# Two-operand work on the mixer's constants: from GpSimd to VectorE, one instruction per weight slot

## The chip, the cores and the metric

One core of a Trainium2 chip runs the whole program. The metric is the device time of one execution in microseconds (us). Engines are called by the names of the profile: PE is TensorE (PEld its weight loads), DVE is VectorE, ACT is ScalarE, POOL is GpSimd, SP the queue that issues the weight loads.

## What is computed

One inference step of two layers for 272 prompt and 32 sample tokens (304 columns in layer 0). Layer 0 mixes by a gated short convolution, layer 1 by a state-space mixer with complex diagonal state; each is followed by an MLP.

```python
def sq_relu_mlp(x, w_up, w_down):
    h = jax.nn.relu(x @ w_up)          # 2048 -> 8192
    return (h * h) @ w_down            # 8192 -> 2048

# constants of the state-space mixer, from weights alone:
dt = jnp.exp(log_step)[:, None]
mag = jnp.exp(lr * dt)
abar_re, abar_im = mag * jnp.cos(li * dt), mag * jnp.sin(li * dt)
q_re = ((abar_re - 1) * lr + abar_im * li) / (lr * lr + li * li)
q_im = (abar_im * lr - (abar_re - 1) * li) / (lr * lr + li * li)
bbar_re = q_re[..., None] * b_re - q_im[..., None] * b_im
bbar_im = q_re[..., None] * b_im + q_im[..., None] * b_re
```

The kernel runs the mixer over blocks of four tokens, and for this needs powers of `abar` and their products with `bbar` and with C. It makes them while the first MLP runs, and stores them to DRAM in the layouts in which layer 1 reads them.

## The kernel before

All weights stream through `WeightStream` (lines 40 to 82) as 704 slots, each one pair of 128x512 tiles (512 KB). For a slot, SP loads `raw` (4 buffers), ACT copies it to `whi` (L66; fp32r, a rounded copy), DVE makes `wlo = raw - whi` (L68); both have 3 buffers and are made two slots ahead (`LOOK = 2`). `group` (from line 172) then issues 24 matmuls for the slot: 4 output tiles x 2 contraction tiles x 3 products (L196 and L197 with `whi`, L198 with `wlo`). A group gathers 4 output tiles in 4 of the 7 PSUM buffers `ps`; in its first slot it leaves the matmuls of the fourth tile to the end, behind the 18 of the other three, since that tile's buffer must first be freed by an eviction of the group before.

The first MLP has 256 slots. Eight column parts `f` of the hidden layer are worked off, part f up before part f-1 down, so that the order is 32 slots up, then 16 down and 16 up in turn, and at the end 16 twice down. Counted from 0, slots 32 to 47 are down, 48 to 63 up, 64 to 79 down, and so on every 32. An up group has 8 slots, a down group 4. Evictions of a finished group run in the first slots of the next: for up, `ev_up` has DVE make `zt` (L836) and `at` (L838), ACT the rounded `hid` (L732), DVE the rest (L733); for down, `h_add` (L794) adds to `h` on DVE. The first of them is issued ahead of the first slot's `whi` and `wlo`, the others one per slot in the middle of it.

The background list `bg` holds the work on the mixer's constants (`prep_tasks`, from line 443), behind 8 empty items. At the end of every slot of the first MLP, `group` takes one item (lines 222 to 232): `None` does nothing, a function is called, and a generator is advanced by one `yield`. In the kernel before, the call that makes a generator uses up a slot of its own. Engines work their instructions in the order of issue; so what an item issues on DVE or ACT stands behind that slot's `wlo` and evictions and ahead of the next slot's. The items in their order: load (`t_alloc`), `exp`, sine and cosine and `abar` on DVE (`t_exp`, `t_trig`, `t_abar`), scaling of B by the norm (`t_wnorm`, L550), powers (`t_pow` by `cmul`, L518 to L523), `a4` by PE transposes (`t_a4`). Then for each of two halves (real, imaginary): four `t_w` of three operations on 128x1024 (L584 to L586), four transposing copies on ACT (`t_wm`, L592), stores to `d_b` and `d_m1` issued by POOL (L596, L601). Then C is loaded and half of it negated (`t_cload`, `t_cneg`), and four sets follow, each with a copy and four `t_m2` of three operations on 128x512 (L636, L640 to L642) and stores to `d_c` and `d_m2` (L648, L651). The profile calls all of these DRAM tensors `d_m`, `d_b`, `d_c`, the SBUF buffers `prep` and `nat`. At the end come 256 small matmuls on the constants (`t_kmm`, L688, 16 in an item), `t_d` (L696, L698, on POOL) and stores to `d_t` (L701).

The views of `t_w` and `t_m2`, whose inputs lie differently:

```python
b = [bg_[:, x * 1024:(x + 1) * 1024].rearrange("g (p c) -> g p c", c=16) for x in range(2)]
e = [nat(16 + 2 * tau + x).unsqueeze(2).to_broadcast([P, 64, 16]) for x in range(2)]

c = [bg_[:, x * 1024:(x + 1) * 1024].rearrange("g (c p) -> g p c", c=16)[:, ps_, :] for x in range(2)]
a = [nat(8 + 2 * (i - 1) + x)[:, ps_].unsqueeze(2).to_broadcast([P, 32, 16]) for x in range(2)]
```

`t_w` reads B with neighbouring elements; `t_m2` reads C with a step of 64 elements; both broadcast one factor along the innermost 16.

Of the kernel before, what the change touches and what calls it, by code (L numbers as in the profile page):

```python
# [11 lines left out]
AF = mybir.ActivationFunctionType  # L12
ALU = mybir.AluOpType
# [3 lines left out]
P = 128  # L17
# [62 lines left out]
def build(ctx, tc, I, O, dbg=None):  # L80
    nc = tc.nc
    V, S, G, T = nc.vector, nc.scalar, nc.gpsimd, nc.tensor
# [62 lines left out]
    bg = []  # L145
# [42 lines left out]
    def group(kts, rhs, n, rate=1, fast=False, each=None):  # L188

        ps = [psum() for _ in range(4)]  # L190

        def mm(m, kk, si, hi, lo):
            xh, xl = rhs(kts[si + kk])
            o = ps[m][:, :n]
            wh, wl = hi[:, kk, m * P:(m + 1) * P], lo[:, kk, m * P:(m + 1) * P]
            T.matmul(out=o, lhsT=wh, rhs=xh, start=si == 0 and kk == 0, stop=False)  # L196
            T.matmul(out=o, lhsT=wh, rhs=xl, start=False, stop=False)  # L197
            T.matmul(out=o, lhsT=wl, rhs=xh, start=False, stop=si + 2 >= len(kts) and kk == 1)  # L198

        for si in range(0, len(kts), 2):  # L200
            while si == 0 and len(tasks) > 3 and tasks[3][2]:
                tasks.pop(0)[1]()
            run_pend()
            hi, lo = W.take()
            if si + 2 >= len(kts):
                order = [(m, kk) for m in range(4) for kk in range(2)]
            else:
                order = [(m, kk) for kk in range(2) for m in range(4 if si else 3)]
                if si == 0:
                    order += [(3, 0), (3, 1)]  # L210
            for m, kk in order[:4]:
                mm(m, kk, si, hi, lo)
            pop_tasks(rate)
            if each is not None:
                each()
            for m, kk in order[4:]:
                mm(m, kk, si, hi, lo)
            if len(tasks) > 5 or fast:
                pop_tasks(rate)
            else:  # L220
                run_pend()
            if bg:
                f = bg[0]
                if hasattr(f, "__next__"):
                    if next(f, bg) is bg:
                        bg.pop(0)
                else:
                    bg.pop(0)
                    if f is not None:
                        it = f()  # L230
                        if hasattr(it, "__next__"):
                            bg.insert(0, it)
        return ps

# [33 lines left out]
    big = rp.tile([P, 12000], F32, tag="BIG", name="big")  # L268
# [178 lines left out]
    def prep_tasks():  # L447
# [9 lines left out]
        def nat(i, n=64):  # L457
            return st["vy"][:, i * 64:i * 64 + n]
# [56 lines left out]
        def cmul(o, a, b):  # L515

            t = nat(4)
            G.tensor_tensor(out=nat(o), in0=nat(a), in1=nat(b), op=ALU.mult)  # L518
            G.tensor_tensor(out=t, in0=nat(a + 1), in1=nat(b + 1), op=ALU.mult)
            G.tensor_tensor(out=nat(o), in0=nat(o), in1=t, op=ALU.subtract)  # L520
            G.tensor_tensor(out=nat(o + 1), in0=nat(a), in1=nat(b + 1), op=ALU.mult)
            G.tensor_tensor(out=t, in0=nat(a + 1), in1=nat(b), op=ALU.mult)
            G.tensor_tensor(out=nat(o + 1), in0=nat(o + 1), in1=t, op=ALU.add)  # L523
# [21 lines left out]

        def t_wnorm():

            for o, n in ((st["big"][:, 0:2048], 128), (nat(30, 16), 1)):
                v = o.rearrange("g (p c) -> g p c", c=16)
                G.tensor_tensor(out=v, in0=v, in1=nat(31, 16).unsqueeze(1).to_broadcast([P, n, 16]), op=ALU.mult)  # L550

        def t_pow():
            cmul(10, 8, 8)
            cmul(12, 10, 8)
            cmul(14, 10, 10)
            for n in range(1, 4):
                cmul(16 + 2 * n, 14 + 2 * n, 8)

        def t_a4():
            ps = psum1()  # L560
# [11 lines left out]
                V.tensor_copy(out=a4[sl, 3, :], in_=im)  # L572

        L += [t_exp, t_trig, t_abar]
        L.extend([t_wnorm, t_pow, None, None, None, None, None, None, None, None, t_a4])

        def t_w(ri, tau):
            bg_ = st["big"]
            b = [bg_[:, x * 1024:(x + 1) * 1024].rearrange("g (p c) -> g p c", c=16) for x in range(2)]
            tmp = bg_[:, 2048:3072].rearrange("g (p c) -> g p c", c=16)  # L580
            wb = bg_[:, 3072:7168].rearrange("g (p t c) -> g p t c", t=4, c=16)
            e = [nat(16 + 2 * tau + x).unsqueeze(2).to_broadcast([P, 64, 16]) for x in range(2)]
            o = wb[:, :, tau, :]
            G.tensor_tensor(out=o, in0=b[ri], in1=e[0], op=ALU.mult)  # L584
            G.tensor_tensor(out=tmp, in0=b[1 - ri], in1=e[1], op=ALU.mult)
            G.tensor_tensor(out=o, in0=o, in1=tmp, op=ALU.subtract if ri == 0 else ALU.add)  # L586

        def t_wm(ri, tau):
            bg_ = st["big"]
# [14 lines left out]
        for ri in range(2):  # L604
            for tau in range(4):
                L.append(lambda ri=ri, tau=tau: t_w(ri, tau))
                L += [None, None]
            L += [None]
            for tau in range(4):
                L.append(lambda ri=ri, tau=tau: t_wm(ri, tau))  # L610
            L += [None, lambda ri=ri: t_wout(ri)]
            L += [lambda ri=ri, a=a: t_m1out(ri, a) for a in range(4)]
            L += [None] * 6
# [5 lines left out]

        def t_cneg():  # L620
            bg_ = st["big"]
            G.tensor_scalar(out=bg_[:, 1024:2048], in0=bg_[:, 1024:2048], scalar1=-1.0, scalar2=None, op0=ALU.mult)

        L.extend([t_cload, None, None, None, t_cneg])

# [4 lines left out]
        def t_m2(ri, hf, i):  # L630
            bg_ = st["big"]
            ps_ = slice(hf * 32, hf * 32 + 32)
            c = [bg_[:, x * 1024:(x + 1) * 1024].rearrange("g (c p) -> g p c", c=16)[:, ps_, :] for x in range(2)]
            o = cbuf(ri, hf)[:, :, i, :]
            if i == 0:
                G.tensor_copy(out=o, in_=c[ri])  # L636
                return
            tmp = bg_[:, 2048:2560].rearrange("g (p c) -> g p c", c=16)
            a = [nat(8 + 2 * (i - 1) + x)[:, ps_].unsqueeze(2).to_broadcast([P, 32, 16]) for x in range(2)]
            G.tensor_tensor(out=o, in0=c[ri], in1=a[0], op=ALU.mult)  # L640
            G.tensor_tensor(out=tmp, in0=c[1 - ri], in1=a[1], op=ALU.mult)
            G.tensor_tensor(out=o, in0=o, in1=tmp, op=ALU.add if ri == 0 else ALU.subtract)  # L642

        def t_m2out(ri, hf, a):
            cb = cbuf(ri, hf)
# [740 lines left out]
```

## Time and profile before

| | |
|---|---|
| median of 3 runs | 2549.51 us (2547.49 to 2554.91) |
| the profiled execution | 2551.72 us, span 2549.9 us |
| mean granted clock of PE | 0.987 of full speed |
| first MLP in the trace | 469.4 us to about 1390 us |

The profile's page gives busy time by engine, the span in 40 slices and the costliest groups. The trace answers for any stretch, line or engine; in its lists of instructions, the bracket at a line's end is the idle time of the engine ahead of the instruction and what ended it. A busy PE is not PE at its peak: its records overlap, so that matmuls per stretch and the granted clock say more than the busy share.

### The profile page before, as it was taken

Reading aid. Unit: us, or ns where it says so; the run is one execution under the profiler, and the core shown is the slowest. Engines: PE = TensorE matmul, PEld = TensorE weight load, DVE = VectorE, ACT = ScalarE, POOL = GpSimd, SP = SyncE. Lnnn points to the kernel's source line nnn. Section 1 sums busy time; section 2 is a strip of 40 time slices with the busy share of each in tenths; the row PEclk is TensorE's granted clock in tenths of the full one; section 3 lists DMA queues with packets and bytes.
Section 4 is the critical chain, followed back from the end, with each engine's and each line's share of the span. In section 5 each row is a group of like instructions: output and inputs, shape, how many; then the busy total and the mean of one; then the engine's idle time right before and its main releaser. Section 6 shows DMA issues by size and latency. Waiting matters only on the chain.

```text
span 2549.9 us, 43295 instructions
## 1 busy us (share of the span) xinstructions
PE 2457.9 (96%) x18078; PEld 2433.5 (95%) x18078; DVE 1469.3 (58%) x2012; ACT 968.1 (38%) x1230; POOL 369.6 (14%) x440
## 2 busy tenths in 40 slices
PE   6999999999989999999989889999999999999998
PEld 5999999999989999999989789999999999999998
DVE  4644555667565774545456983556555545555555
ACT  3333334432424333333323644444333333333334
POOL 2000001016233880000027013000000000000000
PEclk9999999999999999999999999999999999999999
DMA  6555555555656777555569754555555555555554
GB/s 146 154 159 159 160 160 170 157 157 150 174 133 199 209 195 238 160 166 169 162 145 189 139 146 132 166 165 162 170 163 169 163 169 167 166 166 166 165 166 112
DMA packets 256353, 418.17 MB, mean 164 GB/s; under 512 B 64484, under 2 KB 68260, under 8 KB 255980
## 3 DMA queue, kind: packets, MB, share of 16 engines
q1 hardware_dynamic: 248448, 389.62, 52.1%
q0 software_dynamic: 7648, 25.73, 4.9%
q8 instruction: 142, 2.33, 0.4%
q14 instruction: 55, 0.45, 0.1%
q10 hardware_dynamic: 60, 0.05, 0.0%
HBM read 392.71 MB, written 22.63 MB: 163 GB/s over the span
## 4 chain that ended last, share of the span: by engine, by line
PE 58%; DVE 2%; DMA 1%; issue 1%; POOL 0%; ACT 0%; DVEq 0%; ACTq 0%; POOLq 0%
PE ps L196 18%; PE ps L198 18%; PE ps L197 18%; PE ps L1121 1%; DMA raw<-in_mlp_w_down 1%; PE px L688 1%; PE ps L1112 0%; DMA ssm_big<-d_m 0%; DVE ssm_tb L1045 0%; PE ps L1350 0%; DVE wlo L68 0%; DVE ssm_xr L1051 0%; DVE ssm_tb L1046 0%; DVE ssm_xr L1049 0%; PE ps L969 0%
## 5 line engine op out<-in xcount | busy, mean ns | idle before, releaser
L68 DVE TENSOR_TENSOR wlo<-raw,whi 128x1024 fp32r<-128x1024 f32 x701 | 908.7, 1297 | 934.2 <-ACT whi L66 933.5
L66 ACT ACTIVATE whi<-raw 128x1024 fp32r<-128x1024 f32 x704 | 743.2, 1057 | 1034.4 <-PE ps L197 874.7
L196 PE MATMUL ps<-hid,whi 128*128 128x304 f32 (+1 forms) x2048 | 615.8, 301 | 22.8 <-DVE h L794 19.7
L198 PE MATMUL ps<-hid,wlo 128*128 128x304 f32 (+1 forms) x2048 | 615.1, 300 | 9.5 <-DVE wlo L68 9.4
L197 PE MATMUL ps<-hid,whi 128*128 128x304 f32 (+1 forms) x2048 | 615.2, 300 | 0.0
L198 PE MATMUL ps<-xs_m,wlo 128*128 128x304 f32 (+1 forms) x2048 | 611.1, 298 | 1.6 <-DVE wlo L68 1.5
L196 PE MATMUL ps<-xs_m,whi 128*128 128x304 f32 (+1 forms) x2048 | 610.3, 298 | 0.0
L197 PE MATMUL ps<-xs_m,whi 128*128 128x304 f32 (+1 forms) x2048 | 610.2, 298 | 0.0
L196 PEld LDWEIGHTS ps<-hid,whi 128*128 128x128 f32 x2048 | 389.3, 190 | 25.2 <-DVE h L794 20.9
L198 PEld LDWEIGHTS ps<-hid,wlo 128*128 128x128 f32 x2048 | 389.7, 190 | 11.2 <-DVE wlo L68 11.2
L197 PEld LDWEIGHTS ps<-hid,whi 128*128 128x128 f32 x2048 | 388.9, 190 | 0.0
L198 PEld LDWEIGHTS ps<-xs_m,wlo 128*128 128x128 f32 x2048 | 384.6, 188 | 2.4 <-DVE wlo L68 2.4
L196 PEld LDWEIGHTS ps<-xs_m,whi 128*128 128x128 f32 x2048 | 384.6, 188 | 1.2
L197 PEld LDWEIGHTS ps<-xs_m,whi 128*128 128x128 f32 x2048 | 384.5, 188 | 0.1
L196 PE MATMUL ps<-xs,whi 128*128 128x304 f32 x768 | 233.5, 304 | 6.0 <-DVE h L388 6.0
L198 PE MATMUL ps<-xs,wlo 128*128 128x304 f32 x768 | 233.2, 304 | 0.0
L197 PE MATMUL ps<-xs,whi 128*128 128x304 f32 x768 | 232.6, 303 | 0.0
L732 ACT ACTIVATE hid<-at 128x304 fp32r<-128x304 f32 (+1 forms) x128 | 57.8, 452 | 309.8 <-DVE at L838 309.8
L196 PEld LDWEIGHTS ps<-xs,whi 128*128 128x128 f32 x768 | 145.7, 190 | 6.4 <-DVE h L388 6.3
L198 PE MATMUL ps<-g,wlo 128*128 128x288 f32 x512 | 151.1, 295 | 0.0
L196 PE MATMUL ps<-g,whi 128*128 128x288 f32 x512 | 151.1, 295 | 0.0
L197 PE MATMUL ps<-g,whi 128*128 128x288 f32 x512 | 150.7, 294 | 0.0
(283 smaller groups left out, 2450.7 us busy)
## 6 DMA issues: line engine op xcount, KB each, us to landing
raw<-in_mlp_w_up SPq DMA_DIRECT2D x256, 512.0 KB, 3.7
raw<-in_mlp_w_down SPq DMA_DIRECT2D x256, 512.0 KB, 3.6
raw<-in_conv_w_in SPq DMA_DIRECT2D x96, 512.0 KB, 3.8
raw<-in_conv_w_out SPq DMA_DIRECT2D x32, 512.0 KB, 3.6
raw<-in_ssm_glu_w_b SPq DMA_DIRECT2D x32, 512.0 KB, 3.6
raw<-in_ssm_glu_w_a SPq DMA_DIRECT2D x32, 512.0 KB, 3.6
ssm_big<-d_m SPq DMA_DIRECT2D x64, 128.0 KB, 3.0
d_m<-prep POOLq DMA_DIRECT2D x16, 256.0 KB, 8.9
```

What stands on the lines that cost most here:

```text
L66: self.nc.scalar.activation(out=hi, in_=r, func=AF.Copy)
L68: eng.tensor_tensor(out=lo, in0=r, in1=hi.bitcast(F32), op=ALU.subtract)
L196: T.matmul(out=o, lhsT=wh, rhs=xh, start=si == 0 and kk == 0, stop=False)
L197: T.matmul(out=o, lhsT=wh, rhs=xl, start=False, stop=False)
L198: T.matmul(out=o, lhsT=wl, rhs=xh, start=False, stop=si + 2 >= len(kts) and kk == 1)
L688: T.matmul(out=ps[:16, g % 8 * 64:(g % 8 + 1) * 64], lhsT=wl[:, g, :], rhs=cl[:, g, :], start=True, stop=True)
L732: S.activation(out=dh, in_=src, func=AF.Copy)
L1121: T.matmul(out=ps[:NK, n // 2 * P:(n // 2 + 1) * P], lhsT=ssm["SH"][pi][:, 0:NK, n % 2, tl * 4 + n // 2], rhs=ssm["m2"][t % 3][:, n, :], s ...
```

## The change

All two-operand work on the constants up to and with `t_m2` is issued on DVE (`V`) in place of POOL (`G`), `t_cneg` and the copies of `t_m2` on ACT (`S`). The functions become generators that `yield` so that a slot gets about one DVE instruction (two in every second slot of `t_m2`, six small ones in a slot of `t_pow`). A generator now runs its first piece in the slot in which it is made, and many empty items go. The K matmuls and all behind them come 3 slots earlier. DMA issues, memsets and `t_d` stay on POOL.

```diff
                         it = f()
-                        if hasattr(it, "__next__"):
+                        if hasattr(it, "__next__") and next(it, bg) is not bg:
                             bg.insert(0, it)
...
         def cmul(o, a, b):
             t = nat(4)
-            G.tensor_tensor(out=nat(o), in0=nat(a), in1=nat(b), op=ALU.mult)
+            V.tensor_tensor(out=nat(o), in0=nat(a), in1=nat(b), op=ALU.mult)
...
         def t_wnorm():
-            for o, n in ((st["big"][:, 0:2048], 128), (nat(30, 16), 1)):
+            for o, n in ((st["big"][:, 0:1024], 64), (st["big"][:, 1024:2048], 64), (nat(30, 16), 1)):
                 v = o.rearrange("g (p c) -> g p c", c=16)
-                G.tensor_tensor(out=v, in0=v, in1=nat(31, 16).unsqueeze(1).to_broadcast([P, n, 16]), op=ALU.mult)
+                V.tensor_tensor(out=v, in0=v, in1=nat(31, 16).unsqueeze(1).to_broadcast([P, n, 16]), op=ALU.mult)
+                if n > 1:
+                    yield
 
         def t_pow():
...
+            for o, a, b in ((10, 8, 8), (12, 10, 8), (14, 10, 10), (18, 16, 8), (20, 18, 8), (22, 20, 8)):
+                cmul(o, a, b)
+                if o != 22:
+                    yield
...
-        L.extend([t_wnorm, t_pow, None, None, None, None, None, None, None, None, t_a4])
+        L.extend([t_wnorm, t_pow, None, t_a4])
...
-            G.tensor_tensor(out=o, in0=b[ri], in1=e[0], op=ALU.mult)
-            G.tensor_tensor(out=tmp, in0=b[1 - ri], in1=e[1], op=ALU.mult)
-            G.tensor_tensor(out=o, in0=o, in1=tmp, op=ALU.subtract if ri == 0 else ALU.add)
+            V.tensor_tensor(out=o, in0=b[ri], in1=e[0], op=ALU.mult)
+            yield
+            V.tensor_tensor(out=tmp, in0=b[1 - ri], in1=e[1], op=ALU.mult)
+            yield
+            V.tensor_tensor(out=o, in0=o, in1=tmp, op=ALU.subtract if ri == 0 else ALU.add)
...
                 L.append(lambda ri=ri, tau=tau: t_w(ri, tau))
-                L += [None, None]
...
-            G.tensor_scalar(out=bg_[:, 1024:2048], in0=bg_[:, 1024:2048], scalar1=-1.0, scalar2=None, op0=ALU.mult)
+            S.activation(out=bg_[:, 1024:2048], in_=bg_[:, 1024:2048], func=AF.Copy, scale=-1.0)
...
             if i == 0:
-                G.tensor_copy(out=o, in_=c[ri])
+                S.activation(out=o, in_=c[ri], func=AF.Copy)
                 return
...
-            G.tensor_tensor(out=o, in0=c[ri], in1=a[0], op=ALU.mult)
-            G.tensor_tensor(out=tmp, in0=c[1 - ri], in1=a[1], op=ALU.mult)
-            G.tensor_tensor(out=o, in0=o, in1=tmp, op=ALU.add if ri == 0 else ALU.subtract)
+            V.tensor_tensor(out=o, in0=c[ri], in1=a[0], op=ALU.mult)
+            yield
+            V.tensor_tensor(out=tmp, in0=c[1 - ri], in1=a[1], op=ALU.mult)
+            V.tensor_tensor(out=o, in0=o, in1=tmp, op=ALU.add if ri == 0 else ALU.subtract)
...
                     L.append(lambda ri=ri, hf=hf, i=i: t_m2(ri, hf, i))
-                    L.append(None)
+                    L += [None] * (i == 0)
```

The items by slot, from walking the list of each kernel:

| item | before | after |
|---|---|---|
| `t_wnorm`, `t_pow` | 30, 31 | 27 to 29, 30 to 35 |
| `t_w`, real half | 41 to 50 (every third) | 38 to 49 |
| `t_wm`, real half | 54 to 57 | 51 to 54 |
| `t_w`, imaginary half | 70 to 79 (every third) | 67 to 78 |
| `t_wm`, imaginary half | 83 to 86 | 80 to 83 |
| `t_m2`, operations of sets 1 to 4 | 106 to 112, 120 to 126, 134 to 140, 148 to 154 | 103 to 110, 117 to 124, 131 to 138, 145 to 152 |
| first K matmuls | 179 | 176 |

The slot is that in which an item is issued. POOL has nothing there that waits for the slot; it works off its instructions as soon as their inputs are ready.

## Rows read from the trace of the kernel before

**Rows 1.** The page's busy line: engine, busy us, share of the span, instructions.
```profile
PE 2457.9 (96%) x18078; PEld 2433.5 (95%) x18078; DVE 1469.3 (58%) x2012; ACT 968.1 (38%) x1230; POOL 369.6 (14%) x440
```

**Rows 2.** Waits of PE, 390 to 1350 us: us in total, times, longest us.
```profile
PE ps L196 <- DVE h L794: 19.7, 5, 7.3
PE ps L198 <- DVE wlo L68: 10.9, 7, 3.0
PE ps L196 <- DVE zt L836: 2.4, 1, 2.4
```

**Rows 3.** Stretches: length, busy PE, PEld, DVE, ACT, POOL; clock; DMA share, GB/s.
```profile
590.00:600.00 10.00, 5.48 (x30) 5.24 (x30) 9.48 (x6) 3.41 (x4) 9.92 (x5) 0.82 0.33 106
...
800.00:810.00 10.00, 10.00 (x74) 10.00 (x73) 5.31 (x7) 3.94 (x5) 1.13 (x2) 1.00 0.93 276
...
830.00:840.00 10.00, 6.29 (x40) 5.80 (x39) 9.44 (x8) 2.79 (x5) 9.84 (x7) 0.94 0.27 84
...
1000.00:1100.00 100.00, 100.00 (x723) 100.00 (x722) 52.80 (x68) 34.70 (x39) 0.00 (x0) 1.00 0.52 159
```

**Rows 4.** Timeline, 582 to 612 us: start, us, engine, line, operation [idle ahead].
```profile
585.97 2.96 DVE L68 TENSOR_TENSOR wlo<-raw,whi 128x1024 fp32r<-128x1024 f32 x1
...
593.60 2.95 DVE L68 TENSOR_TENSOR wlo<-raw,whi 128x1024 fp32r<-128x1024 f32 x1
595.55 3.22 POOL L586 TENSOR_TENSOR prep<-prep 128x1024 f32<-128x1024 f32 x1
...
596.99 0.62 PE L196 MATMUL ps<-hid,whi 128*128 128x304 f32 x1 [4.52 <-DVE h L794]
```

**Rows 5.** DVE groups, 697 to 725 us, then 1000 to 1100: busy us, mean ns.
```profile
L68 DVE TENSOR_TENSOR wlo<-raw,whi 128x1024 fp32r<-128x1024 f32 x5 | 11.7, 2347 | 6.0 <-ACT whi L66 6.0
...
L68 DVE TENSOR_TENSOR wlo<-raw,whi 128x1024 fp32r<-128x1024 f32 x30 | 36.8, 1226 | 42.6 <-ACT whi L66 42.6
L794 DVE TENSOR_TENSOR h<-h,ps 128x304 f32<-128x304 f32 x14 | 6.5, 465 | 0.0
```

**Rows 6.** Instructions by tile and line: durations min/median/max ns, first and last start.
```profile
L196 PE MATMUL ps<-xs_m,whi x2048: 288/297/528, 469.4 to 2428.3; 128*128 128x304 f32 x94, 128*128 128x288 f32 x93
...
L688 PE MATMUL px<-prep x256: 219/219/230, 1109.0 to 1290.9; 128*16 128x64 f32 x128
```

**Rows 7.** DVE groups of the whole span, by shape: busy us, mean ns.
```profile
L1084 DVE TENSOR_TENSOR ssm_tb<-ssm_tb,ssm_big 128x640 f32<-128x640 f32 x6 | 4.9, 819 | 0.0
...
L485 DVE SCALAR_TENSOR_TENSOR nat<-nat 128x64 f32<-128x64 f32 x7 | 1.6, 223 | 0.2
```

**Rows 8.** Timeline of DVE in an up group's first slots, 1000 to 1060 us.
```profile
1017.10 1.23 DVE L68 TENSOR_TENSOR wlo<-raw,whi 128x1024 fp32r<-128x1024 f32 x1 [0.47 <-ACT whi L66]
...
1020.70 1.23 DVE L68 TENSOR_TENSOR wlo<-raw,whi 128x1024 fp32r<-128x1024 f32 x1 [0.47 <-ACT whi L66]
```

**Rows 9.** Timelines of ACT and PE, 664 to 680 us: `whi` behind `t_wm`.
```profile
670.21 1.05 ACT L66 ACTIVATE whi<-raw 128x1024 fp32r<-128x1024 f32 x1
...
675.77 1.04 ACT L66 ACTIVATE whi<-raw 128x1024 fp32r<-128x1024 f32 x1
...
678.12 0.19 PEld L198 LDWEIGHTS ps<-xs_m,wlo 128*128 128x128 f32 x1 [0.27 <-DVE wlo L68]
```

**Rows 10.** ACT groups of the whole span, by shape: busy us, mean ns.
```profile
L66 ACT ACTIVATE whi<-raw 128x1024 fp32r<-128x1024 f32 x704 | 743.2, 1057 | 1034.4 <-PE ps L197 874.7 <-issue 59.9 <-DMA raw<-in_mlp_w_down 46.8
...
L592 ACT ACTIVATE prep<-prep 128x1024 f32<-128x1024 f32 x8 | 16.6, 2076 | 0.0
```

**Rows 11.** Transfers that write or read `prep`, issue to landing.
```profile
DMA to landing us min/median/max: 2.6/9.4/20.1
```

**Rows 12.** Timeline of ACT behind two bursts of stores: `whi` and its wait.
```profile
694.88 1.06 ACT L66 ACTIVATE whi<-raw 128x1024 fp32r<-128x1024 f32 x1 [5.72 <-DMA raw<-in_mlp_w_down]
...
959.68 1.06 ACT L66 ACTIVATE whi<-raw 128x1024 fp32r<-128x1024 f32 x1 [6.10 <-DMA raw<-in_mlp_w_down]
```

**Rows 13.** Timeline of ACT behind the stores to `d_t`: `whi` and its wait.
```profile
1321.98 1.06 ACT L66 ACTIVATE whi<-raw 128x1024 fp32r<-128x1024 f32 x1 [11.28 <-DMA raw<-in_mlp_w_down]
```

More of the change, by code (lines that the diff above doesn't have):

```diff
@@ L517, in cmul @@
             t = nat(4)
-            G.tensor_tensor(out=nat(o), in0=nat(a), in1=nat(b), op=ALU.mult)
[L519 to L523, printed above, removed]
+            V.tensor_tensor(out=nat(o), in0=nat(a), in1=nat(b), op=ALU.mult)
+            V.tensor_tensor(out=t, in0=nat(a + 1), in1=nat(b + 1), op=ALU.mult)
+            V.tensor_tensor(out=nat(o), in0=nat(o), in1=t, op=ALU.subtract)
+            V.tensor_tensor(out=nat(o + 1), in0=nat(a), in1=nat(b + 1), op=ALU.mult)
+            V.tensor_tensor(out=t, in0=nat(a + 1), in1=nat(b), op=ALU.mult)
+            V.tensor_tensor(out=nat(o + 1), in0=nat(o + 1), in1=t, op=ALU.add)
         def t_abar():
@@ L546, in t_wnorm @@
         def t_wnorm():
-            for o, n in ((st["big"][:, 0:2048], 128), (nat(30, 16), 1)):
+            for o, n in ((st["big"][:, 0:1024], 64), (st["big"][:, 1024:2048], 64), (nat(30, 16), 1)):
                 v = o.rearrange("g (p c) -> g p c", c=16)
-                G.tensor_tensor(out=v, in0=v, in1=nat(31, 16).unsqueeze(1).to_broadcast([P, n, 16]), op=ALU.mult)
+                V.tensor_tensor(out=v, in0=v, in1=nat(31, 16).unsqueeze(1).to_broadcast([P, n, 16]), op=ALU.mult)
+                if n > 1:
+                    yield
         def t_pow():
[L553 to L557, printed above, removed]
+            for o, a, b in ((10, 8, 8), (12, 10, 8), (14, 10, 10), (18, 16, 8), (20, 18, 8), (22, 20, 8)):
+                cmul(o, a, b)
+                if o != 22:
+                    yield
         def t_a4():
```

## The prediction

> **What bounds the kernel now.** TensorE does: in the page's busy line PE has 96% of the span and VectorE 58% [rows 1]. So the question is where PE stands still in the stretch that the change touches, the first MLP. The waits of PE over that stretch [rows 2] name VectorE results: 33.0 us in the three rows, of which the longest single wait, 7.3 us, belongs to a later event (below). The table of stretches [rows 3] shows when: with GpSimd busy 9.8 to 9.9 of 10 us, PE ran 30 and 40 matmuls in 10 us at a granted clock of 0.82 and 0.94; from 1000 to 1100 us, GpSimd idle, it ran 723 in 100 us at clock 1.00 without a gap. So it is GpSimd's arithmetic, 14% of the span, that hurts. How, the timeline shows [rows 4]: the VectorE subtraction that makes `wlo` took 2.96 and 2.95 us beside GpSimd operations, and PE waited 4.52 us for a VectorE result. Grouped by line [rows 5] the same instruction has a mean of 2.347 us beside GpSimd and 1.226 us without it. It is the same work on the same shape: the difference is waiting inside the instruction.
>
> **What that costs.** I count it by slots, since the waits leave out the slow clock after them. A slot is one weight pair, 24 matmuls; 1000 to 1100 us holds 30 of them [rows 5], so 3.333 us each. The first matmul of this MLP starts at 469.4 and the first matmuls on the mixer's constants (L688) at 1109.0 [rows 6]. Walking the list of background items (one per slot, a generator one extra for being made) puts L688 behind slot 179, so 180 slots lie between: 600.0 us unhindered, 639.6 taken. **39.6 us are lost**, waits and slow clock together; three transposes for `a4` and one norm matmul are in it, under 1 us.
>
> **The change, part by part.**
>
> Removed from GpSimd: 24 operations of 128x1024 in `t_w`, 48 of 128x512 and 4 copies in `t_m2`, 36 small ones in `cmul`, `t_wnorm`, `t_cneg`. What stays there is DMA issue, memsets and `t_d`.
>
> Added to VectorE, by its undisturbed durations: 24 + 2 instructions of 128x1024 at 1.23 us [rows 5], 32 us; 48 of 128x512 at 0.69, from the line through 0.819 for 640 elements and 1.226 for 1024 [rows 5, 7], 33 us; 36 of 128x64 at 0.223 [rows 7], 8 us. Together 73 us over 65 slots. Against that, VectorE had 52.8 us of work in 30 clean slots [rows 3], 1.76 per slot, so 1.57 free. One 1.23 us instruction per slot fits on average.
>
> Average is not enough, since VectorE runs in order and an item issued at a slot's end stands ahead of the next `wlo` and the next PSUM eviction. Two kinds of slot:
> - Down groups. ScalarE makes `whi` when the slot begins, so `wlo` starts about 1.1 us in; then come one `h` addition (0.46 [rows 5]) and the new item: 1.1 + 1.15 + 0.46 + 1.23 = 3.9 us, 0.6 into the next slot. The next `wlo` is not due before 1.1 and the first eviction of a new group not before 18 matmuls, 2.5 us. Covered. In the new order `t_w` falls into slots 38 to 49 and 67 to 78, 22 of these 24 in down groups (32 to 47, 64 to 79), so cost nothing.
> - The first four slots of an up group. There `wlo`, `zt`, `at`, ScalarE's `hid`, ScalarE's `whi` and the next `wlo` form a ring, of 3.60 us from `wlo` to `wlo` [rows 8], longer than a slot, with 0.47 us of VectorE idle where the new item falls. An item of 1.23 makes it 4.36, 1.0 late per slot. How late is allowed, rows of before tell: two rings of 5.5 us (2.2 late each) ended in a PE wait of only 0.27 us [rows 9]. So some 4.4 us are free. The worst of the moved work here is the second `t_m2` set, slots 120 to 122: items of 1.38, 0.69, 1.38, lateness 1.2 + 0.5 + 1.2 = 2.9. Covered.
>
> One row speaks against 0.69. ScalarE's copy that reads with a step of 64 elements (L592) takes 2.076 us, its contiguous one of the same size 1.057 [rows 10]. `t_m2`'s products read `c` with that same step, and no VectorE row has such a read. I take 0.69, since the nearest VectorE rows are all without a penalty; the upper bound doubles it to 1.22 for the 32 products, and the three slots are then late by 1.7 + 1.1 + 1.7 = 4.5, a wait of about 0.5 us. I carry 0.5. The Trainium skill, "SBUF — State Buffer", section "Door 1: The DMA port swizzle", says that accesses within one 16-byte line run at full rate and each that crosses to a new line pays. By that rule the upper bound would hold and the sum be the same 0.5 us; the ScalarE rows agree with it, and no VectorE row here tests it.
>
> Moved to ScalarE: `t_cneg` at 1.06 and four strided copies of 512, half of 2.08, 1.04 each [rows 10]. ScalarE has 34.7 us in 100 [rows 3]; one such per 14 slots is inside the 4.4 us.
>
> Moved in time: dropped empty items make everything a few slots earlier, 3 from the K matmuls on. One item lands badly. `t_wm` for the imaginary half, four L592 copies, went to the last two light and first two heavy slots of an up group (as in [rows 9]); now they fall in slots 80 to 83, the first four. Three rings of 5.5 instead of two: 0.27 + 2.2 = **2.5 us of new waits**. DMA issues wait for the same data as before: GpSimd now reaches them without a queue of arithmetic, and VectorE's first write into a stored buffer falls in slot 67, 12 slots or 40 us behind slot 54 where the data was ready; no such store took longer than 20.1 us to land [rows 11].
>
> Not removed: the stores to `d_m1`, `d_m2`, `d_c` crowd the weight loads. ScalarE waited 5.72 and 6.10 us for a load in two such bursts [rows 12], with PE losing matmuls around both. I leave 1.5 us for the first kind (two bursts) and 2.0 for the second (four bursts); from below 0, since one burst left PE at full rate (800 us [rows 3]), from above about 10. And `t_d` with its four stores stays as it is: a load 11.28 us late [rows 13] and the wait of 7.3 us are there again, ten us earlier.
>
> **Sum.** 39.6 - 2.5 - 0.5 - 3.5 = 33.1 us gained. The profiled execution took 2551.7 us (span 2549.9), 2.2 above the median of the three runs shown; 2551.7 - 33.1 - 2.2 = 2516.4. I say **2517**, 1.3% less.
>
> **Rivals.**
> - *All of it goes.* The rings and bursts stay within the 4.4 us of cover: 2549.5 - 39.6 = 2510. For it: a burst with PE at full rate (800 to 810 us, DMA share 0.93 [rows 3]). Against: three slow rings in a row were not in the trace.
> - *Strided reads and bursts together.* Products at 1.22 us make `t_m2` late in up groups while a store burst delays loads, and longer waits bring a slow clock behind them, as the 4.52 us did (0.82 [rows 3, 4]). About 20 us stay: 2530. For it: each burst delayed a load by 5 to 6 us, more than the cover. Against: most bursts fall in slots without items.
> - *No change: the ledger balances.* Beside three `t_w` operations the ring took 7.63 us, from `wlo` at 585.97 to `wlo` at 593.60 [rows 4], against 3.60: 4.0 us lost for three operations, which cost 3.7 us on VectorE itself. If the items ran as close together as on GpSimd, nothing would be won: 2549. Against it: the list now gives one per slot, and most lie in down groups with 1.5 us free. The Trainium skill, "Perfetto Trace Analysis", section "Optimizing Scalar/DVE Operations", warns of just this: the two engines share an SBUF read port, so moving work between them might not help. By that rule the time would be 2549; [rows 4] agree on the port, the count of slots speaks against the conclusion.
> - *Slower: VectorE becomes the bound.* It decides if VectorE's work in a slot, with what its order forces it to wait, exceeds 3.33 us throughout and not only in four slots of an up group. Then each added us lands on PE: 2549.5 + 73 - 39.6 = 2583. For it: rings of 4.36. Against: 1.57 us free per slot, and 3.0 of 3.33 used after.
>
> **How the numbers follow.** Forecast 0.63 (own range 2512 to 2523), all gone 0.15, strided and bursts 0.13, no change 0.05, slower 0.04. 0.3%, some 7.6 us, is what a measurement of this kernel can tell from no change. Faster is the sum of the first three, 0.91. The range goes from 2509, the floor less 1, to 2531: it holds the first three cases but for the tail of the third.
>
> **What would show it.** Right: `wlo` back at 1.23 us in the mean all through the first MLP until `t_d`; no `t_w` or `t_m2` line on GpSimd; L688 first at about 1066 (469.4 + 177 x 3.333 + 6.5); one PE wait of 2 to 3 us on `wlo` near slot 85, around 755 us; VectorE near 9 tenths in the item slots. Wrong: many PE waits on `h` or `zt` at the starts of groups, `t_m2` products above 1 us, clock below 1.0 between 585 and 950, or `wlo` still over 2 us.

## The result, and the profile after

The changed kernel takes 2517.43 us (median of four runs, 2516.69 to 2519.92); the kernel before, on the same chip, 2549.91 us (2547.49 to 2554.91). The ratio is 0.9872, 95% interval 0.9855 to 0.9889: 1.3% faster. Forecast were 2517 and a gain of 33.1 us; 32.5 came. The sum is right, but several of its terms are not, and it is in part luck that their errors cancelled.

The profiled execution of after took 2517.9 us, its span 2516.1 (before 2549.9), at a mean granted clock of 0.991. The page's busy line of after answers to [rows 1]:

```profile
PE 2448.6 (97%) x18078; PEld 2427.3 (96%) x18078; DVE 1477.3 (59%) x2123; ACT 974.2 (39%) x1235; POOL 189.0 (8%) x325
```

GpSimd lost half of its busy time. VectorE took over 85 us of work by the durations in the trace (the prediction had 73) and is only 8 us busier than before: nearly as much as it gained in work it lost in waiting inside its instructions. The groups of VectorE from 575 to 1000 us show that, first the `wlo` row of before, which no group ahead of the prediction has, then those of after (busy us, mean ns, idle ahead):

```profile
L68 DVE TENSOR_TENSOR wlo<-raw,whi 128x1024 fp32r<-128x1024 f32 x116 | 184.3, 1591 | 140.8 <-ACT whi L66 140.7
```

```profile
L68 DVE TENSOR_TENSOR wlo<-raw,whi 128x1024 fp32r<-128x1024 f32 x127 | 155.3, 1224 | 109.8 <-ACT whi L66 108.1 <-PE ps L198 1.6
...
L644 DVE TENSOR_TENSOR prep<-prep,nat 128x512 f32<-128x512 f32 x16 | 17.3, 1081 | 0.0
L642 DVE TENSOR_TENSOR prep<-prep,nat 128x512 f32<-128x512 f32 x16 | 17.1, 1069 | 0.0
...
L645 DVE TENSOR_TENSOR prep<-prep 128x512 f32<-128x512 f32 x16 | 11.1, 692 | 0.6
L585 DVE TENSOR_TENSOR prep<-prep,nat 128x1024 f32<-128x1024 f32 x8 | 9.8, 1220 | 0.0
```

Eleven more `wlo` in the same 425 us, in 29 us less. Now the two landmarks of [rows 6] in after, the first matmul of the MLP and the first on the mixer's constants:

```profile
L196 PE MATMUL ps<-xs_m,whi x2048: 288/297/528, 465.7 to 2393.2; 128*128 128x304 f32 x94, 128*128 128x288 f32 x93
...
L691 PE MATMUL px<-prep x256: 219/219/230, 1060.1 to 1242.0; 128*16 128x64 f32 x128
```

594.4 us for 177 slots, or 590.0 unhindered: **4.4 us lost**, where 39.6 were and 6.5 had been forecast. So 35.2 us of the 33.8 between the two spans were won here. The MLP also starts 3.7 us sooner, and 5.1 us are given back behind L691 (35.2 + 3.7 - 5.1 = 33.8). Of the 3.7, 3.2 are there by the 17th weight pair of the whole program, ahead of all that was changed, and the traces of e1, e7 and e9 have 3.0, 2.3 and 1.8 there too: it is how the one profiled execution of before began. Of the 5.1, some 2.2 lie in the rest of the first MLP, 1.6 right behind it and 1.3 behind the last weights; why is not shown.

What is left of PE's waits from 390 to 1350 us, against three rows in [rows 2]:

```profile
PE ps L196 <- DVE h L797: 11.7, 4, 5.0
```

The four are 1.5 us at 590, 1.7 near 915, and 3.5 and 5.0 behind the stores to `d_t`. The table of stretches puts them in their places (columns as in [rows 3]); between them PE has no gap, with VectorE busy 33 of 40 us in a stretch full of `t_w`:

```profile
580.00:590.00 10.00, 8.75 (x64) 8.51 (x62) 8.68 (x28) 3.77 (x5) 0.00 (x0) 1.00 0.33 110
...
910.00:920.00 10.00, 8.33 (x60) 8.09 (x59) 9.96 (x13) 3.04 (x3) 0.00 (x0) 1.00 0.53 178
...
598.00:638.00 40.00, 40.00 (x291) 40.00 (x290) 33.03 (x37) 12.73 (x12) 2.79 (x1) 1.00 0.70 171
```

**Where the rings lie.** The prediction expected a wait near 755 us, behind the second `t_wm`. The timeline of ACT there shows none (start, us, then the idle time ahead and its end):

```profile
738.09 1.06 ACT L66 ACTIVATE whi<-raw 128x1024 fp32r<-128x1024 f32 x1 [0.30 <-PE ps L197]
739.05 2.10 ACT L595 ACTIVATE prep<-prep 128x1024 f32<-128x1024 f32 x1
741.42 1.06 ACT L66 ACTIVATE whi<-raw 128x1024 fp32r<-128x1024 f32 x1 [0.27 <-PE ps L197]
```

`whi` follows `whi` after 3.33 us, one slot, and waits for PE: ACT is ahead. No `hid` stands between them. Slots 80 to 83 are the first of an up group, but evictions belong to the group that has just *ended*, here a down group, and that gives `h` additions. `zt`, `at` and `hid` come in the four slots *behind* an up group: slots 56 to 59, 64 to 67, 88 to 91, 96 to 99, and so on. In slots 32 to 35 (behind the last group of the first up phase) now stands `cmul`, in the timeline of DVE:

```profile
579.36 1.22 DVE L68 TENSOR_TENSOR wlo<-raw,whi 128x1024 fp32r<-128x1024 f32 x1
580.50 0.47 DVE L839 TENSOR_TENSOR zt<-ps,rstd 128x304 f32<-128x304 f32 x1
581.00 0.48 DVE L841 SCALAR_TENSOR_TENSOR at<-zt 128x304 f32<-128x304 f32 x1
582.00 0.48 DVE L736 TENSOR_TENSOR hid<-at,hid 128x304 fp32r<-128x304 f32 x1 [0.52 <-ACT hid L735]
582.39 0.22 DVE L518 TENSOR_TENSOR nat<-nat 128x64 f32<-128x64 f32 x1
...
583.46 1.22 DVE L68 TENSOR_TENSOR wlo<-raw,whi 128x1024 fp32r<-128x1024 f32 x1
```

From `wlo` to `wlo` 4.10 us, six small operations behind `hid`, against 3.60 [rows 8]. After these slots PE waits 1.5 us. The wait near 915 also stands behind a ring: it has ACT's copy of 1.13 us at 904.29 in it, the third `t_m2` set right behind, and two late loads ahead of it.

**The bursts** cost less here, but not nothing. The waits of ACT for a weight load, 585 to 1000 us (total, times, longest), before and after:

```profile
ACT whi L66 <- DMA raw<-in_mlp_w_down: 25.8, 7, 6.1
ACT whi L66 <- DMA raw<-in_mlp_w_up: 12.5, 4, 4.8
```

```profile
ACT whi L66 <- DMA raw<-in_mlp_w_up: 2.2, 1, 2.2
ACT whi L66 <- DMA raw<-in_mlp_w_down: 1.6, 2, 1.0
```

38.3 us of late loads became 3.8 by this table, although the same stores run. (Two more of after, 2.8 us at 622 and 1.5 near 672, are put down to other engines, though their loads landed just 0.1 us ahead of `whi`.) Both parts of the change had a hand in it: with the new list alone (e1) such waits are 16.7 us, with the new engine alone (e2) 12.9. The 1.6 us on `in_mlp_w_down` lie in the ring ahead of the wait near 915, behind the stores to `d_c` and `d_m` that POOL issued from 884 to 896 us; the timeline of ACT:

```profile
895.98 1.06 ACT L66 ACTIVATE whi<-raw 128x1024 fp32r<-128x1024 f32 x1 [0.61 <-DMA raw<-in_mlp_w_down]
...
900.68 1.06 ACT L66 ACTIVATE whi<-raw 128x1024 fp32r<-128x1024 f32 x1 [1.00 <-DMA raw<-in_mlp_w_down]
...
904.29 1.13 ACT L638 ACTIVATE prep<-prep 128x512 f32<-128x512 f32 x1
```

Seven runs have this same piece of the list: after, e4, e5, e6, e7, e8 and e12. In them ACT's waits for these loads come to 1.61, 1.81, 1.71, 2.25, 2.06, 1.66 and 1.53 us, and PE's wait right behind is 1.67, 1.88, 1.66, 2.31, 2.13, 1.72 and 1.60. So ring, copy and `t_m2` had used up the cover (how late a result may be before PE stands still), and every us of a late load was a us of PE.

### The profile page after: what moved, and what is told of

It is laid out like the page before. It is cut to its first block, busy times and chain, and to the rows that moved or that the text cites. A ratio compares the mean times of both kernels' runs of the same rounds, so it can differ in the third digit from the quotient of the medians.

```text
span 2516.1 us, 43317 instructions
## 1 busy us (share of the span) xinstructions
PE 2448.6 (97%) x18078; PEld 2427.3 (96%) x18078; DVE 1477.3 (59%) x2123; ACT 974.2 (39%) x1235; POOL 189.0 (8%) x325
## 5 line engine op out<-in xcount | busy, mean ns | idle before, releaser
L68 DVE TENSOR_TENSOR wlo<-raw,whi 128x1024 fp32r<-128x1024 f32 x701 | 862.0, 1230 | 888.5 <-ACT whi L66 886.2
```

Source lines behind the costliest of these rows:

```text
L68: eng.tensor_tensor(out=lo, in0=r, in1=hi.bitcast(F32), op=ALU.subtract)
```

## The experiments

Lost is what stands between the first MLP matmul and the first on the mixer's constants, less 3.333 us per slot. Two traces with the same work up to there differ by some 2 us (e7 and e8: 6.5 and 4.5; the difference is the wait near 915, with the clock at 0.83 behind it in e7). The ratio is that to the kernel before on the same chip, whose median was 2552.22 us beside e1 to e4, 2550.28 beside e5 to e8, 2552.53 beside e9 to e11 and 2551.44 beside e12.

| run | start, first K, slots | lost us | median us | ratio, 95% interval |
|---|---|---|---|---|
| e1 list only | 466.2, 1086.6, 177 | 30.4 | 2542.68 | 0.9965 [0.9951, 0.9979] |
| e2 engine only | 466.1, 1080.2, 180 | 14.1 | 2525.31 | 0.9892 [0.9877, 0.9907] |
| e3 t_m2 on GpSimd | 465.7, 1063.1, 177 | 7.4 | 2518.25 | 0.9867 [0.9852, 0.9882] |
| e4 t_w on GpSimd | 465.6, 1085.4, 177 | 29.8 | 2541.46 | 0.9954 [0.9939, 0.9969] |
| e5 idle arithmetic | 466.3, 1074.7, 177 | 18.4 | 2530.31 | 0.9925 [0.9908, 0.9941] |
| e6 idle memsets | 466.2, 1062.8, 177 | 6.6 | 2518.96 | 0.9881 [0.9866, 0.9895] |
| e7 t_d on VectorE | 466.5, 1063.0, 177 | 6.5 | 2507.42 | 0.9833 [0.9819, 0.9848] |
| e8 and paced stores | 465.6, 1060.1, 177 | 4.5 | 2503.72 | 0.9821 [0.9806, 0.9836] |
| e9 and light slots | 467.0, 1040.8, 172 | 0.5 | 2500.74 | 0.9793 [0.9779, 0.9806] |
| e10 t_wm in rings | 465.8, 1064.4, 177 | 8.6 | 2518.25 (one run) | |
| e11 t_m2 unanchored | 467.1, 1066.1, 177 | 9.0 | 2520.98 | 0.9875 [0.9862, 0.9889] |
| e12 t_w in halves | 464.9, 1070.4, 177 | 15.5 | 2527.4 | 0.9907 [0.9891, 0.9924] |

### The two parts of the change alone

The changed list with GpSimd's instructions back (every `V.` of the diff in `cmul`, `t_wnorm`, `t_w`, `t_m2` to `G.`), and the moved instructions with the old list (no `yield`, the old empty items).

> The changed kernel's list (its yields, its order, ScalarE's copies), but all of `cmul`, `t_wnorm`, `t_w` and `t_m2` issued on GpSimd again. Theory A, the loss is VectorE waiting beside GpSimd's arithmetic: it comes back, 2542 to 2551 us, with some 35 to 40 us lost between the start of the first MLP and the first K matmul and a mean of `wlo` over 2 us beside `t_w`. Theory B, the gain came from the order and spacing of the list: 2515 to 2522.

> The list of the kernel before (no yields, three operations in one slot, the empty items), but issued on VectorE, with the copies on ScalarE. Theory A: only the engine counts, and trios of 3.7 us fit into three slots; what is late is `t_pow`, 36 operations or 8 us in one slot ahead of four slots with a ring, some 4 us, and trios of `t_m2` beside rings, 1 to 3: 2520 to 2526. Theory C, one instruction per slot is what makes it work: items of 3 to 8 us in one slot hold up `wlo` and evictions each time, 2535 or more.

Both times lie in A's ranges; e1's loss stays below its 35 to 40. Of 39.6 us lost, the list alone takes away 9.2, the engine alone 25.5, and both 35.2: they add up. With the old list on VectorE, the 36 small operations of `t_pow` stand in one slot, and PE waits 3.3 us for `zt` behind them, at 579. Its other wait for `zt`, 2.7 us at 692, has another cause. The timeline of ACT in e2 shows two loads late behind the eight stores to `d_m` of the real half (issued from 671 to 677 us):

```profile
682.84 1.06 ACT L66 ACTIVATE whi<-raw 128x1024 fp32r<-128x1024 f32 x1 [5.58 <-DMA raw<-in_mlp_w_down]
688.90 1.06 ACT L66 ACTIVATE whi<-raw 128x1024 fp32r<-128x1024 f32 x1 [5.01 <-DMA raw<-in_mlp_w_down]
```

They are the same two weight pairs that were late in before (the second is the first line of [rows 12]), and VectorE was idle for 5.2 and 4.8 us ahead of their `wlo`. From 680 to 700 us 31 matmuls are missing, 4.2 us. So a burst in the wrong place costs PE time without any arithmetic on GpSimd; it was the new list that took this one away. Both parts matter, the engine most.

### Which of the moved work mattered

`t_m2` alone back on GpSimd, then `cmul`, `t_wnorm` and `t_w` alone:

```diff
-            V.tensor_tensor(out=o, in0=c[ri], in1=a[0], op=ALU.mult)
+            G.tensor_tensor(out=o, in0=c[ri], in1=a[0], op=ALU.mult)
```

> The changed kernel with `t_m2` alone back on GpSimd. Theory A: of the 39.6 us lost before, missing matmuls in stretches of 10 us put some 11 into the time of `t_m2`; less the wait of 1.7 that `t_m2` made on VectorE: 2525 to 2530. Theory B: 2517, as the list is unchanged.

> The changed kernel with `cmul`, `t_wnorm` and `t_w` back on GpSimd and `t_m2` left on VectorE. Theory A: some 29 us of the loss lay in their time; less the wait of 1.5 that `cmul` made on VectorE: 2542 to 2547, and what this and the run before lose adds up to the whole. Theory B: 2517.

e3 missed: 2518.25, not distinguishable from the changed kernel, 3.0 us more lost. e4 came out just below its range. So `t_w` with the small operations carries 25 us (29.8 - 4.4), `t_m2` 3, although `t_m2` keeps GpSimd busy longer. First thought: in e3 ACT's copies, which are bound to slots, hold GpSimd's sets in light slots. e11 takes that hold away:

```diff
-            S.activation(out=bg_[:, 1024:2048], in_=bg_[:, 1024:2048], func=AF.Copy, scale=-1.0)
+            G.tensor_scalar(out=bg_[:, 1024:2048], in0=bg_[:, 1024:2048], scalar1=-1.0, scalar2=None, op0=ALU.mult)
...
-                S.activation(out=o, in_=c[ri], func=AF.Copy)
+                G.tensor_copy(out=o, in_=c[ri])
```

> The changed kernel with all of t_m2 and t_cneg on GpSimd, the copies with i = 0 and the negation too, so that nothing on ScalarE holds GpSimd's work to a slot. (With the copies and the negation left on ScalarE, t_m2 on GpSimd cost only 3 us.) Theory A, place decides: GpSimd runs t_m2 as fast as it can, through the rings behind the up groups, the part of the loss that t_m2 had before comes back, 10 to 18 us lost ahead of the first matmuls on the mixer's constants, 2522 to 2531 us. Rival B, t_m2 on GpSimd costs little wherever it lies, because its pieces of 128x512 are short: lost 6 to 9 us, 2517 to 2520 us.

2520.98 and 9.0 lost lie between the two theories, nearest to B: place explains 1.6 us (9.0 - 7.4), less than two such traces differ by, and not 22. Next thought: the length of one GpSimd instruction. e12 is e4 with each `t_w` instruction as two:

```diff
-            G.tensor_tensor(out=o, in0=b[ri], in1=e[0], op=ALU.mult)
+            for h_ in (slice(0, 32), slice(32, 64)):
+                G.tensor_tensor(out=o[:, h_], in0=b[ri][:, h_], in1=e[0][:, h_], op=ALU.mult)
```

> The kernel with cmul, t_wnorm and t_w on GpSimd and t_m2 on VectorE (lost 29.8 us, 2541.5 us), with each 128x1024 instruction of t_w written as two of 128x512: the same elements, the same slots, twice the instructions. What is asked is why t_w on GpSimd costs some 25 us and t_m2 on it only 3 to 5, though t_m2 keeps GpSimd busy longer. Theory A, the length of one GpSimd instruction decides: a wlo that meets one waits about until it ends, and beside t_m2's 128x512 it took 1.9 to 2.4 us, beside t_w's 128x1024 2.96: beside the halves no wlo is over 2.5 us, the loss falls to 8 to 18 us and the time to 2520 to 2531 us. Rival B, it hangs on what the instructions read (t_m2's products read with a step of 64 elements, t_w's do not) or on where they lie, not on their length: some wlo stay at 2.9 us or as many are late, the loss is still 25 us or more, 2537 to 2545 us.

2527.4 and 15.5 lost, as A said: 14 us won by cutting the same work on the same engine in two, though it then takes GpSimd longer (73.2 us for 48 halves, 62.4 for 24 whole ones). The groups of DVE and POOL in e4 from 569 to 712 us, then of POOL in e12 from 568 to 696, then of both in e11 from 780 to 905:

```profile
L68 DVE TENSOR_TENSOR wlo<-raw,whi 128x1024 fp32r<-128x1024 f32 x35 | 63.3, 1817 | 35.2 <-ACT whi L66 35.2
L589 POOL TENSOR_TENSOR prep<-prep 128x1024 f32<-128x1024 f32 x8 | 21.6, 2698 | 0.6
```

```profile
L593 POOL TENSOR_TENSOR prep<-prep 128x512 f32<-128x512 f32 x16 | 24.9, 1571 | 0.0
```

```profile
L68 DVE TENSOR_TENSOR wlo<-raw,whi 128x1024 fp32r<-128x1024 f32 x35 | 64.3, 1844 | 30.6 <-ACT whi L66 30.6
...
L645 POOL TENSOR_TENSOR prep<-prep 128x512 f32<-128x512 f32 x16 | 27.1, 1692 | 1.2
```

The mean of `wlo` says little: it is the same in e4 and e11, which lose 25 and 5 us more than after. The rings tell more, in the timelines of DVE, first two `wlo` in a row in e4, then two in e11:

```profile
576.99 2.96 DVE L68 TENSOR_TENSOR wlo<-raw,whi 128x1024 fp32r<-128x1024 f32 x1
...
584.60 2.95 DVE L68 TENSOR_TENSOR wlo<-raw,whi 128x1024 fp32r<-128x1024 f32 x1
```

```profile
792.58 2.37 DVE L68 TENSOR_TENSOR wlo<-raw,whi 128x1024 fp32r<-128x1024 f32 x1
...
797.94 2.38 DVE L68 TENSOR_TENSOR wlo<-raw,whi 128x1024 fp32r<-128x1024 f32 x1
```

A ring beside `t_w` takes 7.6 us, beside `t_m2` mostly 5.3, once 7.0 (3.60 undisturbed), and in e12, beside the halves of the real half, 4.5 to 5.0. One of A's details failed, that no `wlo` passes 2.5 us beside halves:

```profile
691.96 4.29 DVE L68 TENSOR_TENSOR wlo<-raw,whi 128x1024 fp32r<-128x1024 f32 x1 [0.22 <-ACT whi L66]
```

That one lies beside two halves in a row, as do an `at` of 3.36 us at 665 and a `hid` of 3.27 at 673, where two rings take 7.0 and 6.8 us; in e11 too there is one `wlo` of 4.04. So length decides the amount, but a wait can outlast one GpSimd instruction. Why it does, and why halves still lose 11 us (15.5 - 4.4) where `t_m2` loses 3 to 5, stays open.

### Is it GpSimd's arithmetic, or GpSimd being busy?

The changed kernel with idle work on GpSimd in the clean stretch behind 1000 us, in a region that nothing reads: 16 multiplications of 128x1024, or 40 memsets of 128x1248.

```diff
+            for _ in range(16):
+                G.tensor_tensor(out=r, in0=r, in1=r, op=ALU.mult)
```

> The changed kernel, with 16 two-input GpSimd multiplications of 128x1024 added on a piece of `prep` that nobody else uses, between the first K loads and the K matmuls, where nothing waits for them. Theory A: VectorE's two-input instructions wait beside them as beside `t_w`. Twelve `t_w` operations beside down groups cost 7.6 us, twelve beside an up group's rings about 21; the stretch here is mostly down groups: 2527 to 2537. Rival, the loss came from what waited for GpSimd's results or stood behind it in its queue: 2517.

> As the run before, but with 40 GpSimd memsets of 128x1248 in place of the multiplications, for about the same time: GpSimd busy, writing and reading nothing. Theory A in the narrow form (the two engines get into each other's way in reading): 2517 within 2 us, `wlo` at 1.23. In the wide form (any GpSimd work on SBUF): 2525 or more.

Groups from 1004 to 1041 us in e5, then in e6:

```profile
L714 POOL TENSOR_TENSOR prep<-prep 128x1024 f32<-128x1024 f32 x16 | 36.4, 2272 | 1.3
...
L68 DVE TENSOR_TENSOR wlo<-raw,whi 128x1024 fp32r<-128x1024 f32 x7 | 19.1, 2727 | 2.0 <-ACT whi L66 1.9
```

```profile
L714 POOL MEMSET prep<- 128x1248 f32 x31 | 35.4, 1143 | 1.8
...
L68 DVE TENSOR_TENSOR wlo<-raw,whi 128x1024 fp32r<-128x1024 f32 x12 | 14.7, 1225 | 15.1 <-ACT whi L66 15.1
```

Beside arithmetic `wlo` takes 2.73 us and 14 us are lost; beside memsets that fill as much of these 37 us it takes 1.225, its undisturbed duration, and 2.2 us are lost, about what two such traces differ by. So neither GpSimd being busy nor its writing disturbs. The Trainium skill, "SBUF — State Buffer", section "Who interferes with whom", says so: a VectorE instruction with two SBUF inputs contends with a GpSimd instruction that reads SBUF, not with one that only writes it. Both runs agree. The two runs differ in more than reading, though: the multiplications have two inputs. One instruction on GpSimd that reads with a single input is in e11, the negation `t_cneg`; the timelines of POOL and DVE:

```profile
775.50 3.35 POOL L624 TENSOR_SCALAR prep<-prep 128x1024 f32<-128x1024 f32 x1 [5.96 <-DMA prep<-in_ssm_c_im]
```

```profile
777.32 1.22 DVE L68 TENSOR_TENSOR wlo<-raw,whi 128x1024 fp32r<-128x1024 f32 x1 [1.11 <-ACT whi L66]
```

The `wlo` lies wholly inside it and is not delayed; the same pair in before took 2.79 and 1.24 us. The rule, as far as it speaks of all reading, is not borne out by these two cases. Shown is that two-input arithmetic on GpSimd delays and memsets do not; that any reading does is not shown.

### The rings, tested

e10 moves the second half's `t_wm` by eight empty items, from slots 80 to 83 into 88 to 91, behind an up group; empty items taken out further down keep the later order (the `t_m2` sets come four slots later).

```diff
-            L += [None]
+            L += [None] * (1 + 8 * ri)
```

> The changed kernel with ScalarE's four t_wm copies of the imaginary half moved from slots 80 to 83 (behind a down group) to slots 88 to 91 (behind an up group); the later items keep their order. The prediction had put 2.5 us of waits on these copies at slots 80 to 83; the trace of the changed kernel showed none there. Theory A, the amount was right and the place wrong: three rings of about 5.5 us from whi to whi, and one or two PE waits of 1.5 to 3 us together between 765 and 785 us, lost in all 6 to 7.5 us instead of 4.4. Rival B, the copies are harmless at any place, since two late rings or three are covered: no PE wait over 0.5 us there, lost 4 to 5 us.

The timeline of ACT, then the table of stretches:

```profile
767.36 1.04 ACT L66 ACTIVATE whi<-raw 128x1024 fp32r<-128x1024 f32 x1
770.60 0.46 ACT L735 ACTIVATE hid<-at 128x304 fp32r<-128x304 f32 x1 [2.19 <-DVE at L841]
770.96 2.05 ACT L595 ACTIVATE prep<-prep 128x1024 f32<-128x1024 f32 x1
772.91 1.04 ACT L66 ACTIVATE whi<-raw 128x1024 fp32r<-128x1024 f32 x1
```

```profile
770.00:780.00 10.00, 8.99 (x62) 8.35 (x60) 4.03 (x8) 7.22 (x7) 0.00 (x0) 1.00 0.35 105
780.00:790.00 10.00, 9.29 (x56) 9.19 (x56) 4.34 (x4) 5.41 (x5) 6.06 (x8) 0.83 0.80 198
```

Three rings of 5.55 us. Full rate is 72.3 matmuls in 10 us, so 26.6 are missing over the 20 us, 3.7 us. The waits that the trace names are 1.7 us (1.0 for `whi`, 0.7 for `wlo`), the rest is the clock of 0.83 behind them; no load is late here. So A's place and lateness hold; its lower bound for the waits is just met, and lost is 8.6, above the 6 to 7.5. The price that the prediction gave these copies was about right; they just did not stand there. One run says nothing on the total.

### Towards a faster kernel

e7 moves `t_d` to VectorE, with a `yield` between its two operations; e8 also spreads the four `d_t` stores, six slots apart, on ScalarE's queue, and moves the K matmuls closer together.

```diff
-            G.tensor_tensor(out=ks()[:, :, 0, :], in0=ks()[:, :, 0, :], in1=tmp, op=ALU.add)
+            yield
+            V.tensor_tensor(out=ks()[:, :, 0, :], in0=ks()[:, :, 0, :], in1=tmp, op=ALU.add)
...
-            L += [lambda j=j: t_tout(j), None]
+            L += [lambda j=j: t_tout(j)] + [None] * 5
```

> The changed kernel with `t_d`, the last arithmetic of the list on GpSimd, on VectorE too, in two slots. Two PE waits stand behind it: one of about 3.5 us beside its operations, one of about 5 with a weight load 10 us late behind the stores to `d_t`. If the first is the same contention, 3 to 4 us go: 2513 to 2515. If the stores cause both: 2517.

> As the run before, the K matmuls closer together (two empty items in place of four between pairs) and the four stores to `d_t` issued from ScalarE's queue, six slots apart. If the burst of stores makes the wait that is left, that goes with the slow clock behind it: 2506 to 2510. If each store slows loads enough by itself: 2512 to 2517.

e7 came out 6 us below its range. The table of stretches shows why: two of after, where the two `d_t` waits lie, then the worst of e7, which has the stores unchanged:

```profile
1250.00:1260.00 10.00, 6.49 (x36) 6.25 (x35) 7.11 (x8) 3.41 (x4) 5.22 (x5) 0.83 0.72 73
...
1270.00:1280.00 10.00, 4.96 (x23) 4.81 (x22) 4.82 (x6) 3.17 (x3) 5.28 (x12) 0.66 0.82 259
```

```profile
1280.00:1290.00 10.00, 9.06 (x64) 8.56 (x62) 1.90 (x3) 1.06 (x1) 0.00 (x0) 1.00 0.98 154
```

Its load is still late (the longest of ACT's waits for one is 8.7 us), and PE waits 1.4 us for it. In after, with `t_d` on GpSimd ahead of the same stores, 86 matmuls are missing in those two stretches, 12 us. So here a late load and a VectorE late ahead of it share one cover, and the load without the other is nearly hidden; e2 above shows a place where it is not. e8, 2 us below its range too, took away most of what was left, but its interval overlaps that of e7.

e9 is e8 with empty items that keep `cmul`, `t_wm`, the `t_m2` sets and ACT's copies out of the ring slots as corrected above; all stores of a `t_m2` set are now issued in one slot, and lie elsewhere too.

```diff
+                for _ in range(4 * (o == 12)):
+                    yield
...
+                L += [None] * (4 * (ri == 0 and tau == 1))
...
+            if ri == 0:
+                L += [None] * 11
```

> The kernel with t_d on VectorE and paced stores (the one before this run, lost 4.5 us ahead of the first matmuls on the mixer's constants), with its list shifted by empty items so that cmul, t_wm, the four t_m2 sets and ScalarE's copies keep out of the slots in which the ring of wlo, zt, at, hid and whi runs. Theory A, those rings lie in the first four slots behind an up group, and the two waits left (1.5 us at cmul, 1.7 us at a t_m2 set) come from items that fall into them: both waits go, under 0.5 us is left of them in the first MLP up to 1050 us, 1 to 2.5 us are lost in that stretch, and the time is 2499 to 2503 us. Rival B, the waits come from the amount of added work, wherever it lies, or the rings lie in the first slots of every up group: 3 us of waits stay, lost 4 to 5 us, 2503 to 2506 us.

Theory A: the table of stretches from 560 us on has no gap and no slow clock, with a VectorE as busy as in after,

```profile
560.00:660.00 100.00, 100.00 (x724) 99.96 (x723) 75.57 (x130) 38.71 (x39) 2.79 (x1) 1.00 0.61 167
660.00:760.00 100.00, 100.00 (x723) 100.00 (x722) 65.15 (x78) 45.88 (x42) 14.96 (x17) 1.00 0.72 189
760.00:860.00 100.00, 100.00 (x723) 100.00 (x723) 70.73 (x90) 37.77 (x41) 7.86 (x11) 1.00 0.67 207
860.00:960.00 100.00, 100.00 (x723) 100.00 (x722) 73.96 (x94) 36.63 (x40) 13.41 (x18) 1.00 0.67 200
```

and 0.5 us are lost in 573.3, less than the 1 to 2.5 that A had. Late loads hardly meet a ring any more (one, of 0.7 us at 769), so e9 does not tell what the place of the items gave from what the place of the stores gave. This kernel beats both before, by 2.1%, and after; against e8, measured on another chip, the 3 us are not told apart from none.

## Why the prediction was right, and where its steps failed

- **That GpSimd's arithmetic costs 39.6 us through `wlo`, and that nearly all of it goes**: right. 35.2 went; `wlo` is back at 1.22 us; e1, e2, e5 and e6 show that two-input arithmetic on that engine is the cause. Not all of the 39.6 came through `wlo`: e2 shows one burst that cost 4.2 us without it, which the new list moved. The step took all of the moved work as one, though. e3, e4, e11 and e12 show that `t_w`'s long instructions made most of it and `t_m2` little; the sum did not need that split, a choice of what to move would have.
- **One item of 1.23 us per slot is covered**: right in the down groups. PE ran all 291 matmuls of 598 to 638 us at clock 1.00 with VectorE at 8 tenths. "VectorE near 9 tenths" was a little high.
- **"The first four slots of an up group" hold the ring**: wrong. They are the four slots behind an up group. Two terms hung on it. The 2.5 us for `t_wm` at slots 80 to 83 were 0; e10, with the copies in a true ring, lost 3.7 us there, so the price was fair and the place wrong. And `cmul` in slots 32 to 35, which the prediction passed over, cost a wait of 1.5 us. ACT's copy in slot 129, counted as covered, helped to use up the cover ahead of the wait of 1.7. e9 removed both waits by moving items and stores.
- **The strided products of `t_m2`**: taken at 0.69 us, measured at 1.07 and 1.08, inside the bounds and nearer the upper one (1.22); products above 1 us were among the signs that the prediction gave for being wrong, and this one came. `t_w`'s products, with a broadcast factor but neighbouring elements, took 1.22 for twice the size, so the broadcast costs nothing, and the step takes the time to some 1.55 times that of `t_m2`'s sums (0.69). The 0.5 us carried for it (its own figures, 4.5 late against 4.4 free, give less) covers no wait of its own: the second set, for which it was carried, met none. Whether it has a part in the wait of 1.7 is not separated.
- **The bursts, 3.5 us**: mis-sized. The 1.5 us for the stores to `d_m1` did not come; e2 shows that such a burst costs 4.2 us in its old place, and in after it stands elsewhere. The 2.0 for `d_m2` and `d_c` came at one burst of four: the wait of 1.7 near 915 grows with the late loads one for one, and 2.2 us are lost there (4.4 and 4.2 in e6 and e7, where the granted clock of the 10 us around it was 0.83). The price was right in size and hangs on the place; ring, copy, items and loads share one cover.
- **`t_d` unchanged**: right. 8.5 us of waits against 7.3, a slow clock behind them; moving it off GpSimd was worth 10 us (e7), with the stores and the K matmuls moved as well 14 (e8).
- **No change, because the engines share a port** (the rival with the Trainium skill, "Perfetto Trace Analysis", section "Optimizing Scalar/DVE Operations"): fell. The engines do hold each other up, but the ledger does not balance: 85 us of work on VectorE fill time in which it had nothing due.
- **VectorE as the bound**: fell. It is busy 59% (before 58%), and 0.5 us lost in e9 is compatible with the whole load.

Terms left were 6.5 us in the forecast (2.5 + 0.5 + 3.5); 4.4 were lost, some 2.0 at `cmul`, which had no term, and some 2.2 near 915. The 2.1 us between them are no more than two traces of this list differ by (e7 lost 6.5). The 3.7 us from the earlier start, of which the 2.2 taken off for the profiled execution may be a part, and the 5.1 given back were not forecast. That the total met 2517 so closely is luck.

## What to carry to other kernels

Work that runs beside a saturated engine is priced by the slot that it falls into, not by its sum: list, slot by slot, what the engine already owes there (and to which *finished* group the evictions belong), and put new work where nothing waits. A two-input instruction on GpSimd delays VectorE's two-input instructions, by about its own length and at times by that of two in a row, so cut it short or move it. A late load and an engine late beside it draw on one cover: a stall seen when both are late is not the price of either, and where the stores stand against the heavy slots decides whether their late loads cost anything.

## What the runs showed of the hardware that was not expected

- Memsets on GpSimd leave VectorE's two-input instruction at 1.225 us, multiplications of the same total length take it to 2.73; two negations with a single input (e11, before) left it at 1.22 and 1.24.
- Halving GpSimd's instructions, 24 of 128x1024 to 48 of 128x512, lost 14 us less in spite of 11 us more of GpSimd time.
- VectorE's multiplication with one input at a step of 64 elements takes 1.07 to 1.08 us for 128x512, its two-input addition of neighbouring elements 0.69; ScalarE's copy with such a step doubles [rows 10].
- After 1.7 us of waits in e10 the granted clock of one 10 us stretch was 0.83 in the mean, so a part of it ran at 1.2 GHz instead of 2.4, and more was lost to that than to the waits; single waits of 1.5 and 1.7 us in after left it at 1.00, single ones of 2.1 and 2.3 near 915 in e7 and e6 took it to 0.83.
